# Up weights loaded by quarters into fixed places, the plain block split around the last products, six accumulating transfers for two blocks, and spilled forms read back later

## The chip, the cores and the metric

One core of a Trainium2 chip runs the whole kernel. The metric is device time in microseconds (us); lower is better. Engines are named as in the profile: PE (TensorE), DVE (VectorE), ACT (ScalarE), POOL (GpSimd), SP (SyncE, which here only issues transfers).

## The reference

One layer of a decoder trunk over 512 positions of width 1024: a mixer (mLSTM heads and a convolution group) and then a gated feed-forward block with a causal convolution of width 3. The change lies in the second half:

```
u  = rms_norm(x, ffn_pre_g) * (1 + sc2) + sh2          # 512 x 1024
up = causal_dwconv(u @ ffn_up, ffn_conv_w, ffn_conv_b)  # 1024 -> 2 * 2816, width 3 over positions
a, gt = split(up, 2)
f  = (silu(gt) * a) @ ffn_down                          # 2816 -> 1024
x  = x + g2 * rms_norm(f, ffn_post_g)
```

All is float32. sc2, sh2 and g2 are columns of a modulation that depends on c alone.

## The kernel before

A float32 product is made of three matmuls: each operand is split into a high and a low part (names ending in h and l), and high*high, high*low and low*high are summed (`mm3`, the lines L188 to L190; L1082 in `form_product`). A split is one ACT copy for the high part and a subtraction for the low part, on POOL in `w_split` (weights of the up stage) and on DVE in `split` (activations and down weights). `added_split` makes the low part otherwise: ACT writes the negated high part, and a transfer that POOL issues adds the source to it in place (an accumulating transfer).

**Up stage.** The 2816 hidden columns are 22 units of 128 (i = 0 to 21), each with a "value" and a "gate" block; two units make a pair m, 11 in all. Units 0 to 7 are plain: 48 matmuls of 512 columns. From unit 8 on, the even unit of a pair is a product unit: its blocks are computed by seven products of 12 matmuls of 256 columns (a Strassen-like scheme over halves of the positions and of the contraction), p1, p5, p7, p6 first and p2, p3, p4 last. Between the first four and the last three, DVE adds partial sums together (`u2`, then into the accumulators X and Z; L1106 to L1109), and p2, p3, p4 accumulate on top. The odd unit of the pair is plain, 48 matmuls of 512 columns in two halves (value, then gate), between the first four and the last three products. Before the weights can be multiplied, DVE forms sums of their four quarters in place (L1089, L1090, L1093 for p5, p7, p6; L1114 for p3). Weights for p1 to p7 are split by `w_split`; the plain unit's four by `added_split`. The position side of the products (`tforms`, t1 to t4) is made by `token_forms` after units 4 and 6.

Each unit's result goes through `conv3` (an ACT pass, two DVE passes), the silu and a product into F (L1146); `forms(m, F)` makes four sums (L1021 to L1024) and splits them (fh on ACT L1013, fl on DVE L1014) for the down stage, and sends two blocks to DRAM (`g2d`, L1031 and L1032, from ACT's queue). The forms of pairs 0 to 3 are written out to `own` and read back by 16 transfers of 256 KB on SP's queue before the down weights' first loads.

Up weights come in loads of 1 MB into `raws`, a ring of two tiles, with 20 tiles of split weights in `wpool`. `asides` puts two modulation columns (`ada_block`, a DVE pass of 1024 columns, L155) in front of units 4, 8, 12 and 16; they are ordered on DVE behind an earlier operation, `last_lo`.

**Down stage.** `load1(m)` brings 768 KB of down weights (into the ring's tiles for m = 0, 1, 4, 5, ..., named wd, into the place of u2h, named wdmore, for m = 2, 3, 6, 7, ...), `forms1(m)` makes sums and splits (L1222 to L1224, b_ and t_), and `prod1` runs 24 matmuls of 512 columns for each m.

SP and PE run in the order in which the code is written. The order on ACT, DVE and POOL is chosen by a scheduler when the program is built; each engine then runs its list strictly in order.

Of the kernel before, what the change touches and what calls it, by code (L numbers as in the profile page):

```python
# [25 lines left out]
NF = DFF // P  # L26
# [26 lines left out]
def decoder_layer(ctx, tc, w_glu0, x, xT, c, adaT, vecs, w_glu, w_qko, w_v0, w_v, w_out, w_up, w_down, out):  # L53
    nc = tc.nc
    V, S, G, PE = nc.vector, nc.scalar, nc.gpsimd, nc.tensor
# [41 lines left out]
    def cvbank(name):  # L97
        return cvpool[0].tile([P, T], F32, tag="cv", name=name)
# [48 lines left out]
    def ada_block(i, behind):  # L147

        if i % 6 < 4 and 24 <= i < 40:
            r = spare[0][:, 2 * (i % 6) : 2 * (i % 6) + 2, :].rearrange("p j t -> p (j t)")  # L150
        else:
            r = adas.tile([P, D], F32, tag="ada", name=f"ada_{i}")
        nc.scalar.dma_start(r, adaT[i // 2][:, (i % 2) * D : (i % 2 + 1) * D])
        junk = small.tile([P, D], BF16, tag="junk", bufs=1, name=f"junk_{i}")
        t = V.scalar_tensor_tensor(out=junk, in0=r, scalar=1.0, in1=cb, op0=ALU.mult, op1=ALU.mult, accum_out=mod[:, i : i + 1])  # L155
        tc.add_manual_dep(t.ins, behind.ins.name, mybir.DependencyInfo(mybir.DependencyClass.NoSync, mybir.DependencyReason.DATA),
                          reason="order on VectorE")
# [6 lines left out]
    def w_split(src, name, pool=None, tag="w", eng=None):  # L164

        n = src.shape[1]
        pool = pool or wpool
        hi = pool.tile([P, T], F32R, tag=tag, name=f"{name}h")
        lo = pool.tile([P, T], F32R, tag=tag, name=f"{name}l")
        S.activation(hi[:, :n], src, AF.Copy)  # L170
        (eng or G).tensor_tensor(out=lo[:, :n], in0=src, in1=hi[:, :n].bitcast(F32), op=ALU.subtract)  # L171
        return hi, lo

    def w_load(view, name, pool=None, tag="w"):

        n = view.shape[1]
        r = raws.tile([P, 2048], F32, tag="raw", name=name)
        nc.sync.dma_start(r[:, :n], view)
        return [w_split(r[:, a : min(a + T, n)], f"{name}_{a}", pool, tag) for a in range(0, n, T)]

    def blk(pieces, b):
        hi, lo = pieces[b // 4]
        a = (b % 4) * P
        return hi[:, a : a + P], lo[:, a : a + P]

    def mm3(ps, a, b, start, stop):

        PE.matmul(ps, a[0], b[0], start=start, stop=False)  # L188
        PE.matmul(ps, a[0], b[1], start=False, stop=False)  # L189
        PE.matmul(ps, a[1], b[0], start=False, stop=stop)  # L190
# [104 lines left out]
    _, _, u = u_tiles("u")  # L295
# [693 lines left out]
    def halves(z):  # L989
        return z.rearrange("p (h t) -> p h t", h=2)  # L990

    def conv3(ps, i, name):
        t = cvtile(f"{name}c")
        w = lambda tap: vcol("ffn_conv_w", tap * 44 + i)
        S.activation(t, ps, AF.Identity, bias=vcol("ffn_conv_b", i), scale=w(2))
        for d in range(1, 3):
            V.scalar_tensor_tensor(out=t[:, d:], in0=ps[:, : T - d], scalar=w(2 - d), in1=t[:, d:], op0=ALU.mult, op1=ALU.add)
        return t
# [60 lines left out]
            split(z, hi, lo)  # L1059
            tforms[n] += [tuple(y[:, h * HT : (h + 1) * HT] for y in (hi, lo)) for h in range(2)]  # L1060

    def up_load(i):
        r = raws.tile([P, 2048], F32, tag="raw", name=f"wup{i}")
        nc.sync.dma_start(r, w_up[i])
        return r

    def quarter(r, b):
        return r[:, b * T : (b + 1) * T]

    def added_split(r, i, q):  # L1070

        hi, lo = (wpool.tile([P, T], F32R, tag="w", name=f"wup{i}_{q}{n}") for n in "hl")
        S.activation(hi, quarter(r, q), AF.Copy)
        S.activation(lo, quarter(r, q), AF.Copy, scale=-1.0)
        G.dma_start(lo, quarter(r, q), accum_op=ALU.add)
        return hi, lo

    def form_product(ps, w, b, start, stop):
# [4 lines left out]

    def first_forms(i):

        r = up_load(i)
# [25 lines left out]
    def last_forms(i, r):  # L1112
        a11, a12, a22 = quarter(r, 0), quarter(r, 1), quarter(r, 3)
        V.tensor_tensor(out=a11, in0=a12, in1=a11, op=ALU.subtract)  # L1114
        return [w_split(z, f"wup{i}_{n}") for n, z in (("p2", a12), ("p3", a11), ("p4", a22))]

    def last_products_up(banks, w):
        X, Z = banks
# [1 line left out]
        form_product(X[:, HT:], w[1], B22, False, True)  # L1120
        form_product(Z[:, :HT], w[2], tforms["t4"], False, True)

    def plain_unit(i):
        if i < NE:
            return early[i]
        if i < SUNITS[0]:
            pieces = w_load(w_up[i], f"wup{i}")
            bank = mmbank
        else:
            r = up_load(i)  # L1130
            pieces = [added_split(r, i, q) for q in range(4)]
            bank = cvbank
        both = []
        for half in range(2):
            ps = bank(f"up{i}_{half}")
            for k in range(KT):
                mm3(halves(ps), blk(pieces, half * KT + k), (u2h[:, :, k, :], u2l[:, :, k, :]), k == 0, k == KT - 1)
            both.append(ps)
        return both

    def unit_out(i, banks, F):
        pa, pg = banks
        a = conv3(pa, i, f"fa{i}")
        g = conv3(pg, NF + i, f"fg{i}")
        S.activation(g, g, AF.Silu)
        V.tensor_tensor(out=F[:, (i % 2) * T : (i % 2 + 1) * T], in0=a, in1=g, op=ALU.mult)  # L1146

    def asides(i):
        if i in (4, 8, 12, 16):
            ada_block(38 + i // 2, last_lo[0])  # L1150
            ada_block(39 + i // 2, last_lo[0])
        if i == 18:
            ada_done(40, 48)
            gain(3, 40, "ffn_post_g")
            send_rows(3 * KT, KT)
            wide = adas.tile([P, D], F32, tag="ada", name="g2r")
            g2.append(row(3, lambda n: [wide[:, :T], wide[:, T:]], "g2"))

    g2 = []
    for m in range(NM):  # L1160
        F = vpool.tile([P, 2 * T + 8], F32, tag="vh", name=f"F{m}")
        i = 2 * m
        asides(i)
        if i in SUNITS:
            r, w = first_forms(i)
            banks = first_products(i, w)
            unit_out(i + 1, plain_unit(i + 1), F)
            last_products_up(banks, last_forms(i, r))
            unit_out(i, banks, F)
        else:  # L1170
            for i in (2 * m, 2 * m + 1):
                unit_out(i, plain_unit(i), F)
                if i in (4, 6):
                    token_forms(i // 2 - 2)
        forms(m, F)
        if m < SPILLED:
            for n, pair in enumerate(pairs[m]):
                for e, z in enumerate(pair):
                    nc.scalar.dma_start(own_d[m][:, (2 * n + e) * T : (2 * n + e + 1) * T], z.bitcast(F32))
    g2r = g2[0]  # L1180
    for m in range(SPILLED):
        pairs[m] = [(slot(f"fh{m}_{n}b", F32R), slot(f"fl{m}_{n}b", F32R)) for n in range(2)]
        for n, pair in enumerate(pairs[m]):
            for e, z in enumerate(pair):
                nc.sync.dma_start(z.bitcast(F32), own_d[m][:, (2 * n + e) * T : (2 * n + e + 1) * T])
    pairs = [pairs[m] for m in ORDER]
    g2_d = [g2_d[m] for m in ORDER]
    w_down = [w_down[m] for m in ORDER]

# [24 lines left out]
    def load1(m):  # L1214
        loaded[m] = r = wd_raw(m, 1)
        nc.sync.dma_start(r[:, T:], w_down[m][:, T:])
# [244 lines left out]
```

## Time and profile before

| | |
|---|---|
| median of 3 runs | 819.56 us (818.29 to 820.01) |
| profiled execution | 821.4 us, span 819.4 us |
| PE busy | 766.4 us, 94% |
| DVE busy | 648.2 us, 79% |
| ACT busy | 435.9 us, 53% |
| POOL busy | 380.9 us, 46% |
| moved by DMA | 141.12 MB, mean 172 GB/s |

Busy time is that of the engine's own instructions; issuing transfers is not counted. A wait in square brackets behind a row is the engine's idle time before it, with the operation that ended it. The pairs with a product unit run from 506.56 us to 683.76 us on PE, the down stage starts at 704.69 us.

### The profile page before, as it was taken

The numbers are of one execution on the slowest core, as the hardware profiler recorded it, in microseconds if no ns is written. First come the engines' busy times: TensorE is split into PE (matmuls) and PEld (weight loads), VectorE is DVE, ScalarE is ACT, GpSimd is POOL, SyncE is SP. The second block draws the span as 40 slices with busy tenths as digits, with TensorE's granted clock in tenths as the row PEclk, the third lists the DMA queues.
The fourth block names the chain that finished last, engine by engine and source line by source line (L and its number), as shares of the span: only waits on it lengthen the run. The fifth ranks groups of instructions, "written<-read, shape, count | busy, mean of one in ns | idle before, by whom it ended". The sixth has DMA issues, their size and how long they took to land.

```text
span 819.4 us, 11429 instructions
## 1 busy us (share of the span) xinstructions
PE 766.4 (94%) x3961; PEld 655.5 (80%) x3961; DVE 648.2 (79%) x1039; ACT 435.9 (53%) x832; POOL 380.9 (46%) x315
## 2 busy tenths in 40 slices
PE   7999999999999999999999998989888993699996
PEld 6788898788788889888899887878777883488885
DVE  6979999999998667569587998775656574699895
ACT  4556374866775465714453445555654462355762
POOL 2049495976986444428424776445544450000001
PEclk9999999999999999999999999899989998699998
DMA  9982223131133624268536653565444663877872
GB/s 331 368 290 84 104 82 146 47 109 52 52 130 130 204 102 156 102 226 314 202 132 233 224 174 103 192 174 148 91 137 146 174 157 107 310 279 235 292 245 103
DMA packets 45054, 141.12 MB, mean 172 GB/s; under 512 B 5154, under 2 KB 6594, under 8 KB 39108
## 3 DMA queue, kind: packets, MB, share of 16 engines
q1 hardware_dynamic: 26676, 100.37, 34.6%
q10 hardware_dynamic: 14288, 32.68, 11.2%
q0 software_dynamic: 4032, 7.34, 5.3%
q8 instruction: 31, 0.51, 0.3%
q14 instruction: 27, 0.22, 0.1%
HBM read 117.42 MB, written 15.61 MB: 162 GB/s over the span
## 4 chain that ended last, share of the span: by engine, by line
PE 56%; DVE 22%; DMA 10%; issue 5%; ACT 4%; POOL 2%; SPq 0%; ACTq 0%; DVEq 0%; POOLq 0%
DVE cv L731 10%; PE up L189 5%; PE up L188 4%; PE up L190 4%; PE p L1308 4%; DMA wup<-in_w_up 3%; PE glu L189 3%; PE glu L190 3%; DMA wup_3l<-wup 3%; PE glu L188 3%; PE p L188 3%; PE p L189 3%; PE p L190 3%; PE upx L1082 2%; PE mixa L188 2%
## 5 line engine op out<-in xcount | busy, mean ns | idle before, releaser
L731 DVE SCALAR_TENSOR_TENSOR cv<-gt,cvw,cv 128x505 f32<-128x505 f32 (+24 forms) x200 | 137.4, 729 | 2.3 <-ACT cv L719 1.1
L685 POOL TENSOR_TENSOR ro2r<-ro2t,mhalf 128x1 f32<-128x1 f32 x1 | 0.6, 559 | 132.1 <-DVE ro2t L683 132.1
L727 POOL TENSOR_TENSOR cs<-cs,cs 128x510 f32<-128x510 f32 (+3 forms) x32 | 41.8, 1305 | 0.3
L155 DVE SCALAR_TENSOR_TENSOR junk<-ada,cb 128x1024 bf16<-128x1024 f32 x20 | 30.3, 1516 | 8.5 <-DMA ada<-in_adaT 8.2
L725 ACT ACTIVATE cs<-gt,cvw 128x511 f32<-128x511 f32 (+4 forms) x40 | 27.4, 717 | 6.3 <-POOL cs L727 3.1
L171 POOL TENSOR_TENSOR wup_p1l<-wup,wup_p1h 128x512 fp32r<-128x512 f32 x7 | 9.6, 1376 | 38.5 <-ACT wup_p1h L170 38.5
L1014 DVE TENSOR_TENSOR fl<-F,fh 128x512 fp32r<-128x512 f32 x11 | 11.8, 1073 | 18.2 <-ACT fh L1013 18.2
L189 PE MATMUL up<-u2l,wup_0h 128*128 128x512 f32 (+1 forms) x72 | 25.7, 356 | 0.2 <-DVE u2l L910 0.2
L188 PE MATMUL up<-u2h,wup_0h 128*128 128x512 f32 (+1 forms) x72 | 25.6, 356 | 0.0
L190 PE MATMUL up<-u2h,wup_0l 128*128 128x512 f32 (+1 forms) x72 | 25.4, 353 | 0.0
L171 POOL TENSOR_TENSOR wqko_1024l<-wqko,wqko_1024h 128x512 fp32r<-128x512 f32 x12 | 16.3, 1359 | 18.4 <-ACT wqko_1024h L170 12.9
L171 POOL TENSOR_TENSOR wglu_0l<-wglu,wglu_0h 128x512 fp32r<-128x512 f32 x4 | 5.5, 1386 | 40.8 <-PE glu L190 40.5
L1082 PE MATMUL upx<-u2h,wup_p2h 128*128 128x256 f32 x28 | 9.6, 341 | 16.0 <-DVE upx L1109 9.3
L155 DVE SCALAR_TENSOR_TENSOR junk<-spare,cb 128x1024 bf16<-128x1024 f32 x12 | 19.0, 1586 | 3.4 <-DMA spare<-in_adaT 3.2
L188 PE MATMUL p<-b_0h,fh 128*128 128x512 f32 x2 | 1.4, 714 | 20.9 <-ACT b_0h L1013 20.9
L1082 PEld LDWEIGHTS upx<-u2h,wup_p2h 128*128 128x128 f32 x28 | 6.4, 227 | 18.0 <-ACT wup_p7h L170 7.7
L188 PE MATMUL qko<-uh,wqko_1024h 128*128 128x512 f32 x48 | 20.6, 430 | 0.0
L188 PE MATMUL qko<-uh,wqko_0h 128*128 128x512 f32 x48 | 20.2, 420 | 0.0
L171 POOL TENSOR_TENSOR wup_p5l<-wup,wup_p5h 128x512 fp32r<-128x512 f32 x7 | 9.0, 1282 | 24.0 <-ACT wup_p5h L170 24.0
L276 DVE SCALAR_TENSOR_TENSOR junk<-ada,cb 128x1024 bf16<-128x1024 f32 x16 | 19.5, 1218 | 0.1
L171 POOL TENSOR_TENSOR wo_512l<-wo,wo_512h 128x512 fp32r<-128x512 f32 x8 | 12.9, 1615 | 13.7 <-ACT wo_512h L170 13.7
L171 POOL TENSOR_TENSOR wqko_0l<-wqko,wqko_0h 128x512 fp32r<-128x512 f32 x12 | 16.6, 1384 | 4.9 <-ACT wqko_0h L170 4.8
(1205 smaller groups left out, 3208.3 us busy)
## 6 DMA issues: line engine op xcount, KB each, us to landing
wup<-in_w_up SPq DMA_DIRECT2D x22, 1024.0 KB, 6.9
wqko<-in_w_qko SPq DMA_DIRECT2D x12, 1024.0 KB, 4.8
ada<-in_adaT ACTq DMA_DIRECT2D x20, 512.0 KB, 5.1
ada<-in_adaT SPq DMA_DIRECT2D x16, 512.0 KB, 6.9
wo<-in_w_out SPq DMA_DIRECT2D x8, 1024.0 KB, 4.8
spare<-in_adaT ACTq DMA_DIRECT2D x12, 512.0 KB, 7.3
wd<-in_w_down SPq DMA_DIRECT2D x6, 768.0 KB, 6.4
g2kept<-g2d SPq DMA_DIRECT2D x11, 384.0 KB, 6.0
```

Source lines behind the costliest of these rows:

```text
L155: t = V.scalar_tensor_tensor(out=junk, in0=r, scalar=1.0, in1=cb, op0=ALU.mult, op1=ALU.mult, accum_out=mod[:, i : i + 1])
L171: (eng or G).tensor_tensor(out=lo[:, :n], in0=src, in1=hi[:, :n].bitcast(F32), op=ALU.subtract)
L188: PE.matmul(ps, a[0], b[0], start=start, stop=False)
L189: PE.matmul(ps, a[0], b[1], start=False, stop=False)
L190: PE.matmul(ps, a[1], b[0], start=False, stop=stop)
L276: V.scalar_tensor_tensor(out=junk, in0=first[k][:, i * D : (i + 1) * D], scalar=1.0, in1=cb, op0=ALU.mult, op1=ALU.mult, accum_out=part[k] ...
L725: S.activation(t[:, d:], cvx[j][:, : T - d], AF.Copy, scale=w(CK - 1 - d))
L727: G.tensor_tensor(out=side[:, d:], in0=side[:, d:], in1=t[:, d:], op=ALU.add)
L731: last_tap[0] = V.scalar_tensor_tensor(out=cp[:, d:], in0=cvx[j][:, : T - d], scalar=w(CK - 1 - d), in1=cp[:, d:], op0=ALU.mult, op1=ALU.add)
L1014: behind_turn(V.tensor_tensor(out=lo, in0=src, in1=hi.bitcast(F32), op=ALU.subtract))
L1082: PE.matmul(ps, x, y, start=start and k == 0 and n == 0, stop=stop and k == NT - 1 and n == 2, skip_group_check=True)
L1308: PE.matmul(ps[q], x, y, start=False, stop=m == NM - 1 and i == 2, skip_group_check=True)
```

## The change

- Units 8 and up are loaded by quarters of 256 KB, four transfers for one, into two tiles that belong to them (`wups`, one for even and one for odd units). The even unit's quarters come in the order 0, 2, 3, 1.
- The plain unit of a pair is split: its value half runs between the first four and the last three products, its gate half after the last three. The product unit's result is made before that of the plain unit.
- The splits for p2 and p4 become `added_split` too, so that a pair has six accumulating transfers (four before) and five subtractions on POOL (seven before).
- `token_forms` runs after units 3 and 4 instead of 4 and 6.
- The modulation columns are ordered behind the previous unit's product into F (`gated`) instead of `last_lo`.
- The 16 transfers that read the spilled forms back come after the first three `load1` on SP instead of before them.

```diff
-    def up_load(i):
-        r = raws.tile([P, 2048], F32, tag="raw", name=f"wup{i}")
-        nc.sync.dma_start(r, w_up[i])
-        return r
+    up_raw = []
+
+    def up_load(i, order):
+        if not up_raw:
+            up_raw.extend(raws.tile([P, 2048], F32, tag="raw", name=f"wups{n}") for n in range(2))
+        for q in order:
+            nc.sync.dma_start(quarter(up_raw[i % 2], q), quarter(w_up[i], q))
+        return up_raw[i % 2]
...
-        return [w_split(z, f"wup{i}_{n}") for n, z in (("p2", a12), ("p3", a11), ("p4", a22))]
+        return [added_split(a12, f"wup{i}_p2"), w_split(a11, f"wup{i}_p3"), added_split(a22, f"wup{i}_p4")]
...
+    def plain_half(ps, pieces, off):
+        for k in range(KT):
+            mm3(halves(ps), blk(pieces, off + k), (u2h[:, :, k, :], u2l[:, :, k, :]), k == 0, k == KT - 1)
+        return ps
...
-            ada_block(38 + i // 2, last_lo[0])
-            ada_block(39 + i // 2, last_lo[0])
+            ada_block(38 + i // 2, gated[0])
+            ada_block(39 + i // 2, gated[0])
...
-            r, w = first_forms(i)
-            banks = first_products(i, w)
-            unit_out(i + 1, plain_unit(i + 1), F)
-            last_products_up(banks, last_forms(i, r))
-            unit_out(i, banks, F)
+            j = i + 1
+            r, w = first_forms(i)
+            banks = first_products(i, w)
+            z = up_load(j, range(4))
+            pa = plain_half(cvbank(f"up{j}_0"), [added_split(quarter(z, q), f"wup{j}_{q}") for q in range(2)], 0)
+            ja = conv3(pa, j, f"fa{j}")
+            last_products_up(banks, last_forms(i, r))
+            unit_out(i, conv3(banks[0], i, f"fa{i}"), conv3(banks[1], NF + i, f"fg{i}"), F)
+            pg = plain_half(cvbank(f"up{j}_1"), [added_split(quarter(z, q), f"wup{j}_{q}") for q in range(2, 4)], 0)
+            unit_out(j, ja, conv3(pg, NF + j, f"fg{j}"), F)
...
-                if i in (4, 6):
-                    token_forms(i // 2 - 2)
+                if i in (3, 4):
+                    token_forms(i - 3)
...
     for m in range(3):
         load1(m)
+    for m in range(SPILLED):
+        reload(m)
```

How it moves instructions, at the places that the prediction speaks of. SP where the down stage begins: wd_0, wd_1 and wdmore are the first down weights, fh and fl the spilled forms. Before:

```order
L1185 DMA fl_0b<-own_4552 128x512
L1185 DMA fh_1b<-own_4552 128x512
L1185 DMA fl_1b<-own_4552 128x512
L1216 DMA wd_0_6842<-in_w_down 128x1536
L1216 DMA wd_1_6844<-in_w_down 128x1536
L1216 DMA wdmore<-in_w_down 128x1536
L1226 DMA t2d_4538<-wd_0_6842 128x512
L1216 DMA wdmore<-in_w_down 128x1536
```

and now:

```order
L1068 DMA wups_5123<-in_w_up 128x512 x4
L1220 DMA wd_0_6854<-in_w_down 128x1536
L1220 DMA wd_1_6856<-in_w_down 128x1536
L1220 DMA wdmore<-in_w_down 128x1536
L1188 DMA fh_0b<-own_4549 128x512
L1188 DMA fl_0b<-own_4549 128x512
L1188 DMA fh_1b<-own_4549 128x512
```

All 16 reads of own now stand between the third and the fourth load of down weights (the second wdmore, m = 3).

DVE between pair 14's F and what p2 of pair 16 needs (u_16 is `u2`, upx the accumulator X; junk are the modulation columns). Before:

```order
L1146 TENSOR_TENSOR F_5837<-fa14c,fg14c 128x512
L1021 TENSOR_TENSOR ysum<-F_5837 128x256
L1022 TENSOR_TENSOR F_5837<-F_5837 128x256
L1023 TENSOR_TENSOR ysum<-ysum,F_5837 128x256
L1024 TENSOR_TENSOR ysq<-F_5837,ysum 128x256
L1014 TENSOR_TENSOR fl_0_6064<-F_5837,fh_0_6063 128x512
L1089 TENSOR_TENSOR wup_6328<-wup_6328 128x512
L1014 TENSOR_TENSOR fl_1_6068<-ysum,fh_1_6067 128x512
L1090 TENSOR_TENSOR wup_6328<-wup_6328 128x512
L997 SCALAR_TENSOR_TENSOR fa17c<-up_0_6184,vec,fa17c 128x511
L1106 TENSOR_TENSOR u_16_6107<-upx_6103,p_16_6106 128x256
```

and now:

```order
L155 SCALAR_TENSOR_TENSOR junk_6102,mod<-ada_6100,cb 128x1024
L1021 TENSOR_TENSOR ysum<-F_5857 128x256
L1093 TENSOR_TENSOR wups_5122<-wups_5122 128x512
L155 SCALAR_TENSOR_TENSOR junk_6106,mod<-ada_6104,cb 128x1024
L1022 TENSOR_TENSOR F_5857<-F_5857 128x256
L1023 TENSOR_TENSOR ysum<-ysum,F_5857 128x256
L1094 TENSOR_TENSOR wups_5122<-wups_5122 128x512
L160 TENSOR_TENSOR mod<-mod,vec 128x8
L1024 TENSOR_TENSOR ysq<-F_5857,ysum 128x256
L1014 TENSOR_TENSOR fl_0_6090<-F_5857,fh_0_6089 128x512
L667 SCALAR_TENSOR_TENSOR gains<-mod,vec 128x8
L1014 TENSOR_TENSOR fl_1_6094<-ysum,fh_1_6093 128x512
```

The row behind the last is L1110, u_16. The two junk rows are new there, and the two sums of the next product unit's quarters (L1093 and L1094, before L1089 and L1090) stand wholly in front of u_16.

DVE at the same place for pair 20, the last one. Before:

```order
L1024 TENSOR_TENSOR ysq<-F_6317,ysum 128x256
L1014 TENSOR_TENSOR fl_0_6554<-F_6317,fh_0_6553 128x512
L1014 TENSOR_TENSOR fl_1_6558<-ysum,fh_1_6557 128x512
L997 SCALAR_TENSOR_TENSOR fa21c<-up_0_6666,vec,fa21c 128x511
L1106 TENSOR_TENSOR u_20_6589<-upx_6585,p_20_6588 128x256
```

and now:

```order
L1226 TENSOR_TENSOR wd_0_6854<-wd_0_6854 128x512
L1024 TENSOR_TENSOR ysq<-F_6349,ysum 128x256
L1014 TENSOR_TENSOR b_0l<-wd_0_6854,b_0h 128x512
L1227 TENSOR_TENSOR wd_0_6854<-wd_0_6854 128x512
L1014 TENSOR_TENSOR fl_0_6592<-F_6349,fh_0_6591 128x512
L1014 TENSOR_TENSOR fl_1_6596<-ysum,fh_1_6595 128x512
L1228 TENSOR_TENSOR wd_0_6854<-wd_0_6854 128x512
L1110 TENSOR_TENSOR u_20_6629<-upx_6625,p_20_6628 128x256
L1014 TENSOR_TENSOR t_0l<-wd_0_6854,t_0h 128x512 x2
L1111 TENSOR_TENSOR upz_6626<-upz_6626,u_20_6629 128x256
L1113 TENSOR_TENSOR upx_6625<-upx_6625,u_20_6629 128x256
```

The forms of the first down weights (L1226 to L1228 and the low parts b_0l and t_0l) now run among the forms of pair 18 and ahead of the sums that p2 of unit 20 waits for.

More of the change, by code (lines that the diff above doesn't have):

```diff
@@ L1060, in token_forms, with added_split @@
             tforms[n] += [tuple(y[:, h * HT : (h + 1) * HT] for y in (hi, lo)) for h in range(2)]
-    def up_load(i):
-        r = raws.tile([P, 2048], F32, tag="raw", name=f"wup{i}")
-        nc.sync.dma_start(r, w_up[i])
-        return r
+    up_raw = []
[5 more added lines that the diff above has]
+        return up_raw[i % 2]
     def quarter(r, b):
         return r[:, b * T : (b + 1) * T]
[L1070 to L1075, printed above, removed]
+    def added_split(src, name):
+        hi, lo = (wpool.tile([P, T], F32R, tag="w", name=f"{name}{n}") for n in "hl")
+        S.activation(hi, src, AF.Copy)
+        S.activation(lo, src, AF.Copy, scale=-1.0)
+        G.dma_start(lo, src, accum_op=ALU.add)
         return hi, lo
@@ L1084, in first_forms @@
     def first_forms(i):
-        r = up_load(i)
+        r = up_load(i, (0, 2, 3, 1))
         a11, a21, a22 = quarter(r, 0), quarter(r, 2), quarter(r, 3)
@@ L1125, in plain_unit, with unit_out @@
             return early[i]
[L1126 to L1144, printed above, removed]
+        pieces = w_load(w_up[i], f"wup{i}")
+        return [plain_half(mmbank(f"up{i}_{half}"), pieces, half * KT) for half in range(2)]
+    gated = [None]
+    def unit_out(i, a, g, F):
         S.activation(g, g, AF.Silu)
-        V.tensor_tensor(out=F[:, (i % 2) * T : (i % 2 + 1) * T], in0=a, in1=g, op=ALU.mult)
+        gated[0] = V.tensor_tensor(out=F[:, (i % 2) * T : (i % 2 + 1) * T], in0=a, in1=g, op=ALU.mult)
     def asides(i):
         if i in (4, 8, 12, 16):
-            ada_block(38 + i // 2, last_lo[0])
-            ada_block(39 + i // 2, last_lo[0])
+            ada_block(38 + i // 2, gated[0])
+            ada_block(39 + i // 2, gated[0])
         if i == 18:
@@ L1180, in decoder_layer, with reload @@
     g2r = g2[0]
-    for m in range(SPILLED):
-        pairs[m] = [(slot(f"fh{m}_{n}b", F32R), slot(f"fl{m}_{n}b", F32R)) for n in range(2)]
-        for n, pair in enumerate(pairs[m]):
+    def reload(m):
+        pairs.append([(slot(f"fh{m}_{n}b", F32R), slot(f"fl{m}_{n}b", F32R)) for n in range(2)])
+        for n, pair in enumerate(pairs[-1]):
             for e, z in enumerate(pair):
                 nc.sync.dma_start(z.bitcast(F32), own_d[m][:, (2 * n + e) * T : (2 * n + e + 1) * T])
-    pairs = [pairs[m] for m in ORDER]
+    pairs = pairs[SPILLED:]
     g2_d = [g2_d[m] for m in ORDER]
```

3 lines of the change are left out of this document (2 added, 1 removed).

## The prediction

> **What bounds the kernel now.** I read the page first, then the waits of TensorE over the stage that the change touches, then the timeline rows around those waits.
>
> ```profile
> span 819.4 us, 11429 instructions
> PE 766.4 (94%) x3961; PEld 655.5 (80%) x3961; DVE 648.2 (79%) x1039; ACT 435.9 (53%) x832; POOL 380.9 (46%) x315
> ```
>
> PE is busy for 94% of the span, so the most that can be won is PE's idle time, and it matters where that lies. The waits of PE between 430 and 720 us (total, times, longest):
>
> ```profile
> PE p L188 <- ACT b_0h L1013: 20.9, 1, 20.9
> PE upx L1082 <- DVE upx L1109: 9.3, 3, 4.0
> PE upx L1082 <- ACT wup_p5h L170: 6.7, 2, 3.7
> PE upx L1082 <- ACT t1h L1013: 1.8, 1, 1.8
> PE upx L1082 <- DVE t1l L1014: 1.5, 1, 1.5
> ```
>
> One hole of 20.9 us where the down stage starts, and 19.3 us in seven small ones inside the seven pairs (a product unit with its plain unit). PE's own rows give the pace and the borders (start, duration):
>
> ```profile
> 506.11 0.39 PE L189 MATMUL up<-u2l,wup_1536h 128*128 128x512 f32 x1
> 506.34 0.39 PE L190 MATMUL up<-u2h,wup_1536l 128*128 128x512 f32 x1
> 506.56 0.28 PE L1082 MATMUL upx<-u2h,wup_p1h 128*128 128x256 f32 x1
> 506.68 0.28 PE L1082 MATMUL upx<-u2l,wup_p1h 128*128 128x256 f32 x1
> 605.24 0.55 PE L1082 MATMUL upx<-u2h,wup_p2h 128*128 128x256 f32 x1 [3.99 <-DVE upx L1109]
> 605.59 0.42 PE L1082 MATMUL upx<-u2l,wup_p2h 128*128 128x256 f32 x1
> 605.81 0.41 PE L1082 MATMUL upx<-u2h,wup_p2l 128*128 128x256 f32 x1
> 683.48 0.28 PE L1082 MATMUL upz<-t4h,wup_p4l 128*128 128x256 f32 x1
> ```
>
> The pitch is 0.12 us for a 256-column matmul and 0.227 for a 512-column one, so a pair without waits costs 84 x 0.12 + 48 x 0.227 = 21.0 us. Seven pairs would take 147; from 506.56 to 683.76 (the last row's end) they took 177.2, which is 25.3 each. Of the 30.5 us lost, 19.3 are waits; the other 11.2 are slower running behind them: after the 3.99 us wait the pitch is 0.22 and not 0.12.
>
> What makes the period 25.3 us is a loop through the weight loads:
>
> ```profile
> 588.25 0.87 POOL L1075 DMA_DIRECT2D wup_3l<-wup  x1 [0.74 <-ACT wup_p2h L170]
> 593.23 1.83 SPq L1064 DMA_DIRECT2D wup<-in_w_up  x2
> 599.07 0.63 ACT L170 ACTIVATE wup_p1h<-wup 128x512 fp32r<-128x512 f32 x1 [4.00 <-DMA wup<-in_w_up]
> 600.25 1.38 DVE L1014 TENSOR_TENSOR fl<-F,fh 128x512 fp32r<-128x512 f32 x1 [2.74 <-ACT fh L1013]
> 602.75 0.41 DVE L1106 TENSOR_TENSOR u<-upx,p 128x256 f32<-128x256 f32 x1
> ```
>
> The plain unit's last accumulating transfer (issued 588.25) lands at about 593.2; only then may both 1 MB loads issue; ACT's next p1h waits for one; fh is queued behind p1h on ACT; fl waits for fh on DVE; the u sum (L1106) comes after fl; and p2 waits for that at 605.24.
>
> **The change, part by part.**
>
> *Quarters in fixed places.* This cuts the loop: a quarter of a tile can be loaded as soon as that quarter has been read. The new loop, from one p2 to the next: p2, p3, p4 and 12 matmuls of the plain unit's second half until the tiles for the p4 split come free, 36 x 0.12 + 12 x 0.227 = 7.0; two ACT copies 1.2 (0.6 each, like p1h above); issue and landing of p4's accumulating transfer; the fourth quarter's load; then on DVE two subtractions and fl (0.6 to 0.7 each) and three 256-column operations (0.4 each), 3.0. The transfers' rows (KB, median us to landing), all between 500 and 720 us but the last, which is the page's:
>
> ```profile
> wup_0l<-wup POOLq DMA_DIRECT2D x7, 256.0 KB, 3.4
> wup_3l<-wup POOLq DMA_DIRECT2D x7, 256.0 KB, 5.1
> own<-fl ACTq DMA_DIRECT2D x4, 256.0 KB, 2.3
> fh_0b<-own SPq DMA_DIRECT2D x4, 256.0 KB, 4.7
> wup<-in_w_up SPq DMA_DIRECT2D x12, 1024.0 KB, 6.9
> wd<-in_w_down SPq DMA_DIRECT2D x6, 768.0 KB, 6.4
> ```
>
> No quarter load of up weights exists before; its bounds are 2.3 and 4.7 us. The loop is then 7.0 + 1.2 + 3.4 + 2.3 + 3.0 = 16.9 at best and 7.0 + 1.2 + 5.1 + 4.7 + 3.0 = 21.0 at worst. The pair itself is 21.0, so by itself the loop stalls nothing, but the worst leaves no room.
>
> *What stands in that loop on DVE.* An operation on DVE with both inputs in SBUF gets longer beside a POOL subtraction:
>
> ```profile
> 589.18 3.06 DVE L1146 TENSOR_TENSOR F<-fa13c,fg13c 128x512 f32<-128x512 f32 x1
> 595.10 0.69 DVE L1146 TENSOR_TENSOR F<-fa12c,fg12c 128x512 f32<-128x512 f32 x1 [0.76 <-ACT fg12c L1145]
> 588.81 1.63 POOL L171 TENSOR_TENSOR wup_p2l<-wup,wup_p2h 128x512 fp32r<-128x512 f32 x1
> L171 POOL TENSOR_TENSOR wup_p5l<-wup,wup_p5h 128x512 fp32r<-128x512 f32 x7 | 9.0, 1282 | 24.0 <-ACT wup_p5h L170 24.0
> ```
>
> That is 2.4 us for one hit (3.06 for 0.69); a POOL subtraction by itself takes 1.3 (the last row, the page's: busy, then mean ns). Taking the upper loop, since its transfers will be as crowded as now, one hit on the chain is a wait of 2.4; it does not fall there each time, so I take half, 1.2, for pairs 10, 14 and 18: 3.6.
>
> *The modulation columns.* The eight L155 operations now follow the previous unit's F product, two at a time, ahead of the u sum of pairs 8, 12 and 16. Their row (ns min/median/max):
>
> ```profile
> L155 DVE SCALAR_TENSOR_TENSOR junk<-ada,cb x8: 1214/1438/1974, 433.6 to 461.0; 128x1024 bf16<-128x1024 f32 x8
> ```
>
> Two cost 2.9 us. Pairs 12 and 16: 1.2 + 2.9 = 4.1 each, 8.2. Where they run now, no wait of PE in the list above lies behind them, so I credit nothing there.
>
> *Pair 8.* In the new order p2 follows p1, p5, p7, p6 and only half of the plain unit: 506.56 + 48 x 0.12 + 24 x 0.227 = 517.8. Today DVE makes p2's inputs for that pair here:
>
> ```profile
> 527.08 0.42 DVE L1106 TENSOR_TENSOR u<-upx,p 128x256 f32<-128x256 f32 x1 [0.27 <-ACT p L1105]
> 527.95 0.42 DVE L1109 TENSOR_TENSOR upx<-upx,u 128x256 f32<-128x256 f32 x1
> ```
>
> With nothing else changed p2 would wait until 528.4, 10.6 us. The earlier token forms take the t1 waits (1.8 and 1.5) away and eight DVE operations out of this stretch (5.2), and two L155 come in: 10.6 - 5.2 + 2.9 = 8.3. The ends: 3.0, if a hit goes too and the L155 lie off the chain, and 13.5, if the eight were off it.
>
> *Pair 20.* Six of the first down weights' DVE operations (L1226, b_0l, L1227, L1228, two t_0l, 0.6 each) now precede the last of p2's inputs: 1.2 + 3.6 = 4.8.
>
> *Sum in the up stage.* Waits 3.6 + 8.2 + 8.3 + 4.8 = 24.9, against 19.3 before. Slow running behind them: at least four waits with 12 matmuls at 0.22 instead of 0.12, 4.8; in before's proportion (11.2 for 19.3) 14.5; middle 9.7. Up stage 147 + 24.9 + 9.7 = 181.6, which is 4.4 more than now: at the place where it waits, the change trades one late thing for another.
>
> *Two more accumulating transfers and two POOL subtractions fewer per pair* cost ACT two copies (1.2 us of a 21 us pair, and it is busy 53% of the span) and POOL nothing (0.9 of issue for 1.3 of subtraction): zero off the chain; the copies on the chain are counted above.
>
> *The reads later.* Now the reloads hold the first down loads back; before's SP rows:
>
> ```profile
> 691.19 0.32 SPq L1185 DMA_DIRECT2D fl_1b<-own  x1
> 695.18 0.38 SPq L1185 DMA_DIRECT2D fl_1b<-own  x1
> 695.74 0.99 SPq L1216 DMA_DIRECT2D wd<-in_w_down  x2
> ```
>
> With wd_0 and wd_1 first, their forms are made in pair 20 and the hole of 20.9 goes. What is late next is m = 3: SP first waits with m = 2's load for u2h, that is for the end of the up stage, then issues 16 reloads (nine rows from 691.19 to 695.18, 0.5 each: 8.0), then m = 3's load, 6.4 to landing, 2.0 for its first forms: 17 us behind the stage's end with the issue. PE comes to m = 3 after 3 x 24 x 0.227 = 16.3. That wait is 1 at the least. At the most a reload waits for a transfer, as these SP waits show:
>
> ```profile
> SPq L1185 <- DMA g2d<-ysq: 15.0, 3, 6.9
> SPq L1185 <- DMA g2d<-F: 13.9, 2, 8.3
> ```
>
> One such wait (8.3) makes it 9. The last pair's g2d stores are again under way just then, so I take 7. DVE gives the rest: pair 20's outputs, which ran alone before (6.5 us busy in the hole), now run beside the first forms, and it has little room there:
>
> ```profile
> 684.00:705.00 21.00, 0.31 (x1) 0.29 (x1) 6.52 (x13) 2.98 (x5) 0.00 (x0) 0.62 0.67 235
> 720.00:760.00 40.00, 40.00 (x178) 33.13 (x177) 36.98 (x63) 23.08 (x42) 0.00 (x0) 1.00 0.77 258
> ```
>
> (PE, PEld, DVE, ACT, POOL busy; granted clock; DMA share; GB/s.) DVE at 92%: 2 us of waits of a few tenths. The low clock behind the hole, 0.62 there, comes back behind the wait at m = 3 and cancels.
>
> Total: +4.4 - 20.9 + 7 + 2 = -7.5. The profiled execution took 821.4 (2.0 around its span), so 813.9; the median of the runs lies 1.8 below the profiled one: **812 us**.
>
> **Rivals.**
> *All covers hold.* Only pair 8 waits (8.3 and 1.2 of pace): up 156.5, 20.7 less; the tail as above: -20.7 - 20.9 + 7 + 2 = -32.6, **787**. For it: neither of the loop's two bounds lies over 21.0, and two POOL subtractions fewer can hit DVE. Against: today's fl waited 2.7 for ACT and then ran 1.4 instead of 0.7, and L155 and the down weights' forms now stand in the same line. The Trainium skill ("SBUF — State Buffer", shared port pair) says that a DVE operation with two SBUF inputs and a GpSimd operation that reads SBUF block each other for the whole instruction; the 3.06 us row agrees, and by that rule 14 subtractions fewer would win at most 14 x 1.3 = 18 us, an estimate.
>
> *The loop is longer than the pair, each time (slower).* Place: the fourth quarter's load, ahead of u on DVE. If the worst transfers, a hit (2.4) and ACT's fh being late as in the row above (2.7) fall together, the period is 26.1, and pair 8 waits 10.6: up 32.8 + 6 x 26.1 + 2 x 2.9 + 3.6 = 198.8, +21.6; tail -20.9 + 9 + 2: **831**. It decides from an up stage of about 187 on (26.7 a pair), where the tail's gain is used up. For it: DVE order and four issues for one. Against: 256 KB rows land in 2.3 to 5.1, 1 MB in 6.9. The Trainium skill ("DMA: Bandwidth & Descriptors", Bandwidth) advises 1 MiB or more for each transfer, which speaks for this rival; no run here yet shows an up load of 256 KB, and the down stage draws 258 GB/s, more than a pair needs.
>
> *The tail gives nothing back.* The reloads meet both late transfers (8.3 + 6.9) and m = 3 waits 16: 4.4 - 20.9 + 16 + 2 = +1.5, **821**.
>
> **How the numbers follow.** Forecast 0.56 (804 to 818 by its own bounds: pair 8 at 3.0 or 13.5, pace at 4.8 or 14.5, m = 3 at 1 or 9, not all at one end), all covers hold 0.12, loop too long 0.20, no tail gain 0.12 (a third of it slower by over 0.2%, which is about what a measurement of this kernel can tell from no change). So faster 0.68, the first two; slower 0.20 + 0.04 = 0.24; same 0.08. The range 796 to 824 leaves out most of the second case and the upper part of the third.
>
> **What would show it.** In the changed trace: no wait of PE at the first b_0h; a wait of PE in the down stage's first 25 us, for b_3 or DVE behind wdmore; waits at p2 of pairs 8, 12, 16 and 20 longer than at 10, 14, 18; ACT's p1h without a 4 us wait for a load. Wrong I am if pairs run at 21 to 22 us (then far faster), or if p2 waits over 4 us in pairs without L155 (then slower).

## The result, and the profile after

The changed kernel takes 828.08 us (median of 4 runs, 826.08 to 830.35) against 819.78 for the one before: ratio 1.0106, 95% interval 1.0072 to 1.0139. It is slower by about 1%; the forecast was 812 and faster. Its profiled execution has a span of 828.6 us, 9.2 longer than before.

TensorE's waits from 430 us on (total, times, longest) say where. (In the rows of this document, SPq, ACTq and POOLq mark transfers that the engine issues; the time of such a row is the issue, not the transfer.)

```profile
PE upx L1086 <- DVE upx L1113: 33.1, 6, 14.1
PE p L188 <- ACT b_3h L1013: 9.1, 1, 9.1
PE upx L1086 <- ACT fa11c L995: 3.9, 1, 3.9
PE p L188 <- DVE fg21c L997: 0.5, 1, 0.5
PE upz L1086 <- DVE fg6c L997: 0.2, 1, 0.2
```

The hole of 20.9 us at the first b_0h is gone, and 9.1 came back at m = 3. The waits inside the seven pairs grew from 19.3 us, 16.0 of them at p2, to 37.0, all at p2. PE's rows show which pairs, and the border to the down stage:

```profile
532.15 0.55 PE L1086 MATMUL upx<-u2h,wup_p2h 128*128 128x256 f32 x1 [14.12 <-DVE upx L1113]
559.60 0.55 PE L1086 MATMUL upx<-u2h,wup_p2h 128*128 128x256 f32 x1 [3.92 <-ACT fa11c L995]
587.50 0.55 PE L1086 MATMUL upx<-u2h,wup_p2h 128*128 128x256 f32 x1 [4.42 <-DVE upx L1113]
636.08 0.36 PE L1086 MATMUL upx<-u2h,wup_p2h 128*128 128x256 f32 x1 [3.93 <-DVE upx L1113]
662.56 0.36 PE L1086 MATMUL upx<-u2h,wup_p2h 128*128 128x256 f32 x1 [3.66 <-DVE upx L1113]
692.03 0.55 PE L1086 MATMUL upx<-u2h,wup_p2h 128*128 128x256 f32 x1 [6.76 <-DVE upx L1113]
704.19 0.39 PE L190 MATMUL up<-u2h,wup_3l 128*128 128x512 f32 x1
704.42 0.39 PE L188 MATMUL p<-b_0h,fh 128*128 128x512 f32 x1
730.78 0.79 PE L188 MATMUL p<-b_3h,fh 128*128 128x512 f32 x1 [9.14 <-ACT b_3h L1013]
```

These are pairs 8, 10, 12, 16, 18, 20; pair 14 hardly waits (0.2 us). The first pair starts at 506.20, so the up stage lasts 198.2 us, 21.0 more than before. The balance closes: +21.0 in the up stage, -20.9 at the hole, +9.1 at m = 3, together +9.2, which is the difference of the spans.

The loop that I worked out for the forecast can be read, for one turn, from the p2 of pair 16 (636.08, above) to that of pair 18 (662.56):

```profile
645.70 0.62 ACT L1077 ACTIVATE wup_p4h<-wups 128x512 fp32r<-128x512 f32 x1
646.22 0.62 ACT L1078 ACTIVATE wup_p4l<-wups 128x512 fp32r<-128x512 f32 x1
647.25 1.07 POOL L1079 DMA_DIRECT2D wup_p4l<-wups  x1
654.92 1.38 SPq L1068 DMA_DIRECT2D wups<-in_w_up  x3
659.73 0.69 DVE L1094 TENSOR_TENSOR wups<-wups 128x512 f32<-128x512 f32 x1 [2.46 <-DMA wups<-in_w_up]
660.34 0.69 DVE L1014 TENSOR_TENSOR fl<-ysum,fh 128x512 fp32r<-128x512 f32 x1
661.14 0.40 DVE L1110 TENSOR_TENSOR u<-upx,p 128x256 f32<-128x256 f32 x1
661.99 0.42 DVE L1113 TENSOR_TENSOR upx<-upx,u 128x256 f32<-128x256 f32 x1
```

From p2 to p4's copies 9.6 us, the copies and the way to POOL 1.6, the accumulating transfer until SP goes on 7.7, the quarter's load until DVE goes on 4.8, DVE to the next p2 2.8: 26.5 us, against 21.0 that a pair takes on PE. It is not the same each time: from p2 to p2 the five turns from pair 8 to pair 18 took 27.5, 27.9, 23.4, 25.2 and 26.5 us, 26.1 in the mean. In the short one, which ends at pair 14, DVE's L1094 did not wait for a load. SP's waits from 500 to 735 us name p4's transfer too (first row, total, times, longest). The transfers in that stretch (KB, median us to landing):

```profile
SPq L1068 <- DMA wup_p4l<-wups: 31.9, 6, 6.4
wups<-in_w_up SPq DMA_DIRECT2D x48, 256.0 KB, 5.6
wup_p4l<-wups POOLq DMA_DIRECT2D x7, 256.0 KB, 6.6
wup_3l<-wups POOLq DMA_DIRECT2D x7, 256.0 KB, 6.0
```

### The profile page after: what moved, and what is told of

Same layout as the page of the kernel before. It is cut to its first block, busy times and chain, and to the rows that moved or that the text cites. A ratio compares the mean times of both kernels' runs of the same rounds, so it can differ in the third digit from the quotient of the medians.

```text
span 828.6 us, 11531 instructions
## 1 busy us (share of the span) xinstructions
PE 769.2 (93%) x3961; PEld 656.9 (79%) x3961; DVE 642.3 (78%) x1039; ACT 444.9 (54%) x846; POOL 372.9 (45%) x315
## 4 chain that ended last, share of the span: by engine, by line
PE 56%; DVE 20%; DMA 10%; issue 6%; ACT 4%; POOL 2%; SPq 0%; ACTq 0%; DVEq 0%; POOLq 0%
DVE cv L731 10%; PE up L189 4%; PE up L190 4%; PE up L188 4%; PE p L1314 4%; PE upx L1086 4%; DMA wup_p4l<-wups 3%; PE glu L189 3%; PE glu L188 3%; PE glu L190 3%; DMA wups<-in_w_up 2%; PE glu L316 2%; PE p L189 2%; PE p L188 2%; PE p L190 2%
## 5 line engine op out<-in xcount | busy, mean ns | idle before, releaser
L1086 PE MATMUL upx<-u2h,wup_p2h 128*128 128x256 f32 x28 | 11.3, 405 | 37.0 <-DVE upx L1113 33.1
L171 POOL TENSOR_TENSOR wup_p5l<-wups,wup_p5h 128x512 fp32r<-128x512 f32 x7 | 9.0, 1292 | 52.3 <-ACT wup_p5h L170 46.1
L189 PE MATMUL up<-u2l,wup_0h 128*128 128x512 f32 (+1 forms) x72 | 25.7, 356 | 0.2 <-DVE u2l L910 0.2
L171 POOL TENSOR_TENSOR wqko_1024l<-wqko,wqko_1024h 128x512 fp32r<-128x512 f32 x12 | 15.5, 1293 | 18.3 <-ACT wqko_1024h L170 12.9
L1013 ACT ACTIVATE fh<-F 128x512 fp32r<-128x512 f32 x11 | 6.9, 628 | 27.3 <-DVE F L1022 14.1
L171 POOL TENSOR_TENSOR wo_512l<-wo,wo_512h 128x512 fp32r<-128x512 f32 x8 | 12.9, 1617 | 13.4 <-ACT wo_512h L170 13.4
L190 PE MATMUL qko<-uh,wqko_1024l 128*128 128x512 f32 x48 | 18.8, 392 | 0.0
L190 PE MATMUL qko<-uh,wqko_0l 128*128 128x512 f32 x48 | 18.8, 391 | 0.0
```

The costliest lines, as they stand in the source:

```text
L1086: PE.matmul(ps, x, y, start=start and k == 0 and n == 0, stop=stop and k == NT - 1 and n == 2, skip_group_check=True)
```

## The experiments

Theory A: p2's inputs stand too far back in the lines of ACT and DVE (modulation passes, transfers that ACT issues, the first down weights). Theory B: the loop through p4's accumulating transfer and the fourth quarter's load is longer than a pair. The tail (m = 3) is a question of its own. All ratios are to the kernel before on the same chip, whose median there was 821.4 to 821.8 us; the changed kernel's is 1.0106. Spans are those of the profiled executions. The changed kernel's profiled execution took 830.35 us, 2.3 more than its median, so a difference of spans against it can be some 2 us off.

### The modulation passes early (e1)

```diff
-            ada_block(38 + i // 2, gated[0])
+            ada_block(38 + i // 2, last_lo[0])
```

(and the line after it likewise.)

> The changed kernel, but the eight modulation passes (L155) and their transfers are ordered behind last_lo again, as before the change, and so run ahead of the product pairs. Theory A (what PE waits for at p2 stands in line on ACT and DVE: L155 and the transfers that ACT issues for it): the wait at p2 of pair 8 falls from 14.1 us to 5 to 8, those of pairs 12 and 16 from 4.4 and 3.9 to under 1.5; with the slow running behind them the time falls by 10 to 16 us, to 812 to 818. Theory B (the loop through p4's accumulating transfer and the fourth quarter's load is longer than a pair): pairs 12 and 16 still wait 3 to 4 us as pairs 10 and 18 do, only pair 8 falls by the two passes, 2.4 us; the time falls by 2 to 5 us.

Measured: 822.96 us, ratio 1.0013 (0.9991 to 1.0035), span 821.7. The waits at p2:

```profile
532.10 0.55 PE L1086 MATMUL upx<-u2h,wup_p2h 128*128 128x256 f32 x1 [10.38 <-DVE upx L1113]
557.41 0.36 PE L1086 MATMUL upx<-u2h,wup_p2h 128*128 128x256 f32 x1 [2.83 <-ACT fa11c L995]
582.47 0.35 PE L1086 MATMUL upx<-u2h,wup_p2h 128*128 128x256 f32 x1 [2.35 <-ACT fa13c L995]
607.71 0.35 PE L1086 MATMUL upx<-u2h,wup_p2h 128*128 128x256 f32 x1 [2.52 <-ACT fa15c L995]
631.00 0.36 PE L1086 MATMUL upx<-u2h,wup_p2h 128*128 128x256 f32 x1 [2.06 <-ACT fa17c L995]
655.38 0.55 PE L1086 MATMUL upx<-u2h,wup_p2h 128*128 128x256 f32 x1 [3.04 <-DVE upx L1113]
```

With the passes gone the pairs 10 to 18 all wait 2.1 to 3.0 us, pair 14 too, which had hardly waited. That is a loop's picture, Theory B; the rows stand 23.3 to 25.3 us apart. Pair 8 fell by 3.7 and the span by 6.9, both between the two expectations; pairs 12 and 16 wait 2.4 and 2.1, less than Theory B said and more than Theory A. The passes do cost time, also where they now run: the pairs start 3.0 us later, at 509.22. But they were not why the ordinary pair waits.

### p2 and p4, or p4 alone, split on POOL again (e2, e6)

```diff
-        return [added_split(a12, f"wup{i}_p2"), w_split(a11, f"wup{i}_p3"), added_split(a22, f"wup{i}_p4")]
+        return [w_split(a12, f"wup{i}_p2"), w_split(a11, f"wup{i}_p3"), w_split(a22, f"wup{i}_p4")]
```

e6 changes p4 alone.

> The changed kernel, but p2 and p4 are split by POOL subtractions again: four accumulating transfers for a pair. Theory B: p4's low part is ready 1.3 us after its high part instead of 6.6 us after the issue, the fourth quarter's load is issued about 5 us earlier, DVE's L1094 no longer waits for it, and the waits of pairs 10 and 18 (3.9 and 3.7 us) fall under 1; the time falls by 8 to 12 us. Theory A: these waits stay within 1.5 us, the time changes by less than 3 us, or grows because two more POOL subtractions lengthen DVE operations.

> The changed kernel, but p4 alone is split by a POOL subtraction again, p2 still by an accumulating transfer (five for a pair). If the gain of 13.7 us with both back on POOL comes from the loop through p4's transfer (6.6 us) to the fourth quarter's load: the time is within 3 us of 814. If p2's transfer, or the number of them, matters as much: the time is 819 or more.

Measured: e2 814.39 us, ratio 0.9899 (0.9868 to 0.9930), span 813.2; e6 817.14 us, ratio 0.9960 (0.9943 to 0.9978), span 815.0. Of 15.4 us of span, p4 alone brings 13.6; by the ratios to before it is 12.0 of 17.0. So p4 is most of it, though e6's time is just outside the 3 us around 814, and e2 won more than the 8 to 12 expected. In e2:

```profile
555.89 0.36 PE L1086 MATMUL upx<-u2h,wup_p2h 128*128 128x256 f32 x1 [1.42 <-ACT wup_p7h L170]
579.38 0.36 PE L1086 MATMUL upx<-u2h,wup_p2h 128*128 128x256 f32 x1 [2.25 <-DVE upx L1113]
625.95 0.36 PE L1086 MATMUL upx<-u2h,wup_p2h 128*128 128x256 f32 x1 [2.42 <-DVE upx L1113]
wups<-in_w_up SPq DMA_DIRECT2D x48, 256.0 KB, 4.1
```

Pairs 14 and 18 wait 0.2, pair 10 waits 1.4, and only 12 and 16, which have the modulation passes in line, wait more. In e2 and in e6 DVE's L1094 waits for no load in any of the turns from pair 8 to pair 18. In e6 these five turns take 23.7 us in the mean, so 12.0 of its 13.6 us are won there. The quarter's load itself became 1.5 us faster (4.1 for 5.6). This settles it for pairs 10 to 18: Theory B made the steady wait, and the transfer that closes the loop is p4's. What remains at pairs 12 and 16 is Theory A's share (e12 below).

### The loads in one piece (e5)

```diff
-        for q in order:
-            nc.sync.dma_start(quarter(up_raw[i % 2], q), quarter(w_up[i], q))
+        nc.sync.dma_start(up_raw[i % 2], w_up[i])
```

> The changed kernel, but the up weights of each unit from 8 on come in one load of 1 MB into the fixed place instead of four of 256 KB. Theory B (loop: p4's accumulating transfer, then the load, then DVE): the load now has to wait for the same transfer and lands in 6.9 instead of 5.6 us, so pairs 10 to 18 wait about 1 us longer each (15.9 to 21) and the time grows by 4 to 10 us. Rival (it is the number of transfers that hurts: four issues for one on SP, transfers that ACT issues queued behind them, which held fh for 14.6 us in three places): those holds on ACT go, pairs 8 and 12 wait 5 us less each, and the time falls by 8 us or more.

Measured: 840.16 us, ratio 1.0235 (1.0200 to 1.0271), span 838.7, so 10.1 worse than the changed kernel, at the upper end of what Theory B said; the waits of pairs 10 to 18 came to 25.7 us, more than its 21. SP's waits from 500 to 720 us name the transfer:

```profile
SPq L1067 <- DMA wup_p4l<-wups: 138.2, 6, 28.7
SPq L1067 <- DMA wup_3l<-wups: 34.0, 6, 9.6
```

Loading by quarters is therefore a good part of the change, worth some 10 us beside the rest of it. p4's transfer itself landed in 3.9 us here instead of 6.6, but the whole megabyte now waits for it. The rival fails: no wait of ACT's fh is put down to a load here, and yet pair 8 waits 13.4 and pair 12 10.9 us.

### The reads (e3, e4)

e3 spreads them in the changed kernel:

```diff
-    for m in range(SPILLED):
-        reload(m)
     for m in range(NM):
...
+        if m < SPILLED:
+            reload(m)
```

The second pair of lines stands behind `load1(m + 3)` and `load_g2(m)`. e4 takes the kernel before and makes only the change's move, the reads behind the first three `load1`.

> The changed kernel, but each of the four spilled pairs is read back after one of the next four loads of down weights (behind load1(3) and on) instead of all 16 transfers in front of load1(3). If the wait of 9.1 us at m = 3 is the 16 reads standing in front of that load on SP: the wait goes to under 2 us and the time falls by 7 to 9 us, to 819 to 821. Rival (DVE, 92% busy in the steady down stage and with pair 20's outputs still to make, is what is late): a wait of 4 us or more remains among m = 2 to 5, and the time falls by less than 5 us.

> The kernel before with one part of the change alone: the reads of the spilled forms behind the first three loads of down weights. If the tail's part works by itself as in the changed kernel: the up stage stays at 177 us, the hole of 20.9 us at the first b_0h goes to under 3, a wait of 8 to 10 appears at m = 3, the time falls by 8 to 13 us, to 807 to 812. Rival (the down weights' loads find their ring tiles free only when the last pair has read its up weights, so they are as late as now): a hole of 8 us or more stays at the first b_0h beside the wait at m = 3, and the time falls by less than 4 us.

Measured: e3 819.23 us, ratio 0.9966 (0.9949 to 0.9983), span 818.0; no wait is left at m = 3, whose load SP issues at 701.85 here and at 722.26 in the changed kernel. e4 821.26 us, ratio 1.0006 (0.9980 to 1.0031), span 817.5: no gain, though by neither of the ways that I had written down. Its PE waits in the last pair and behind it:

```profile
687.61 0.55 PE L1082 MATMUL upx<-u2h,wup_p2h 128*128 128x256 f32 x1 [8.32 <-DVE upx L1109]
693.23 0.28 PE L1082 MATMUL upz<-t4h,wup_p4l 128*128 128x256 f32 x1
719.10 0.80 PE L188 MATMUL p<-b_3h,fh 128*128 128x512 f32 x1 [9.24 <-ACT b_3h L1013]
```

The hole of 20.9 us went whole, the up stage ended 9.7 us later (693.51; 683.76 before), with a new wait of 8.3 in pair 20, and 9.2 appeared at m = 3. So the move by itself gives nothing: what it takes from the start of the down stage it gives to pair 20, where the first down weights' forms now stand in front, and to the fourth load.

### Three pairs spilled (e7)

```diff
-    SPILLED = 4
+    SPILLED = 3
```

> The changed kernel, but the forms of pair 3 stay in SBUF: three pairs are written out and read back (12 reads, and no stores by ACT between pair 3's forms and unit 8's p15). If ACT's issue of these four stores holds the copies that DVE's sum for p2 of pair 8 needs: that wait falls from 14.1 us by 4 to 7. If it is the load loop or DVE there: by less than 2. The wait at m = 3 falls by the four reads, 2 us, in either case. Time 828 less 6 to 9, or less 2 to 4.

Measured: 817.55 us, ratio 0.9949 (0.9923 to 0.9976), span 815.9. Pair 8's wait fell from 14.1 to 8.6 and that at m = 3 from 9.1 to 7.0, as expected; the time fell more than the 6 to 9 expected (the span by 12.7): the up stage also lost 3.4 us of slow running and 0.9 of other waits. The changed kernel's ACT rows in pair 8, with the DVE row that writes fh's input, show the queue that this shortens; PE had been ready for p2 since 518.0:

```profile
519.53 3.80 ACTq L153 DMA_DIRECT2D ada<-in_adaT  x2
521.51 0.41 DVE L1022 TENSOR_TENSOR F<-F 128x256 f32<-128x256 f32 x1
523.38 0.63 ACT L1013 ACTIVATE fh<-F 128x512 fp32r<-128x512 f32 x1 [6.75 <-DMA wups<-in_w_up]
525.01 0.33 ACTq L1181 DMA_DIRECT2D own<-fh  x1
525.39 0.63 ACT L1013 ACTIVATE fh<-ysum 128x512 fp32r<-128x512 f32 x1 [1.38 <-DMA wups<-in_w_up]
527.08 0.33 ACTq L1032 DMA_DIRECT2D g2d<-ysq  x1
527.72 0.33 ACTq L1181 DMA_DIRECT2D own<-fl  x1
528.14 0.40 ACTq L1181 DMA_DIRECT2D own<-fh  x1
529.65 0.33 ACTq L1181 DMA_DIRECT2D own<-fl  x1
530.02 0.38 ACT L1106 ACTIVATE p<-upx 128x256 f32<-128x256 f32 x1 [4.00 <-DMA g2d<-ysq]
530.30 0.38 ACT L1109 ACTIVATE p<-upw 128x256 f32<-128x256 f32 x1
```

The two fh and the two p15 copies (p) are computations that need no transfer. Most of the first fh's 6.75 us is not the queue's doing: DVE, behind the two modulation passes, writes its input F only until 521.92, so the issue of the second ada holds it for 1.5 at the most. The second fh and p15 wait 1.38 and 4.00 us because a store in front of them on ACT's queue waits for another transfer. In e7, without four of these stores, the first fh starts 0.7 us earlier and p15 5.7 us earlier (524.30), and 5.5 us of pair 8's wait are gone.

### The plain unit whole again (e9)

```diff
+            pg = plain_half(cvbank(f"up{j}_1"), ...)
             last_products_up(banks, last_forms(i, r))
             unit_out(i, conv3(banks[0], i, f"fa{i}"), conv3(banks[1], NF + i, f"fg{i}"), F)
-            pg = plain_half(cvbank(f"up{j}_1"), ...)
```

> The changed kernel, but the plain unit is not split: both its halves run between the first four and the last three products, as before the change. If the single late things (pair 8's and pair 20's sums for p2) are what the split exposes: p2 comes 24 matmuls, 5.4 us, later in its pair, and the waits of pairs 8 and 20 fall from 14.1 and 6.8 by about 5 each, the others (3.7 to 4.4) little, because the load loop takes as long wherever p2 stands: time 815 to 821. If the split is what shortens the loop (half of the plain unit's tiles free only after p4): pairs 10 to 18 wait more than now, and the time is 826 or more.

Measured: 834.17 us, ratio 1.0153 (1.0120 to 1.0186), span 832.0. A miss in the time for the first expectation, half right in the picture; the time is in the second one's range, but not by its reason. Pair 8 waits 9.1, 5.0 less, as expected; pairs 10 to 18 together 15.5, as with the split (15.9): the loop takes as long wherever p2 stands. But pair 20 waits 12.1 instead of 6.8, and PE waits 2.4 us at the start of the down stage. The up stage is as long as with the split (507.45 to 705.08, 197.6 us). The DVE rows show why pair 20 lost what pair 8 won: DVE waits 5.4 us there for the first down load (L1226 at 684.35) and runs 13 operations of the first two down loads before the X sum at 698.05; with the split it was six.

### Together (e8, e10, e11, e12)

e8 is e2 and e3. e10 adds an order on ACT and DVE alone: the forms of the first two down loads come behind unit 20's p15 copies and its X sum (`after_op` is an order without a wait, as in `ada_block`).

```diff
-        V.tensor_tensor(out=t3, in0=b22, in1=b12, op=ALU.subtract)
+        after_op(V.tensor_tensor(out=t3, in0=b22, in1=b12, op=ALU.subtract), lastx[0], "order on VectorE")
...
+        if early_down[0]:
+            after_op(c, lastp[0], "order on ScalarE")
+            after_op(s, lastx[0], "order on VectorE")
```

e11 adds `SPILLED = 3`, e12 the early modulation passes.

> Two edits together: p2 and p4 split by POOL subtractions, and the reads spread behind the next four loads of down weights. If the two losses are separate, the gains add: 828.1 less 13.7 less 8.9 is 805.5; expected 803 to 808, which beats both kernels. If the shorter up stage only lets the down stage wait elsewhere (for loads, or for DVE): 809 or more.

> The combination of e8, and the forms of the first two down loads ordered behind unit 20's sums on DVE and behind its p15 copies on ACT. If these forms, made early, are what p2 of unit 20 waits for: its wait of 5.6 us falls to under 1.5, the down stage starts without a new wait, and the time falls by 5 to 7 us from 806.7, to 800 to 802. If the forms are then late for the down stage: a wait of 3 us or more appears at b_0 or b_1 and the time is 804 or more.

> The same as e10 with three pairs spilled instead of four. If ACT's stores of pair 3 hold p15 of pair 8 here too (5.1 us on a store in e8): that wait falls from 13.1 to 7 to 9, and the time by 4 to 7 us from e10's. If not: less than 2.

> The same as e11 with the modulation passes back behind last_lo, ahead of the product pairs. In e8 only pairs 12 and 16, where two passes stand in line, still wait (2.3 and 2.4), pairs 14 and 18 do not. If it is these passes: both waits go to under 0.5, pair 8's falls by 2 to 4, the pairs' start is some 3 us later, and the time falls by 4 to 7 us from e11's. If the passes only fill DVE time that is lost anyway: less than 2.

| | median us | ratio to before (95%) | span |
|---|---|---|---|
| e8 | 806.68 | 0.9823 (0.9804 to 0.9842) | 804.8 |
| e10 | 798.82 | 0.9727 (0.9704 to 0.9751) | 797.0 |
| e11 | 794.32 | 0.9665 (0.9637 to 0.9693) | 792.2 |
| e12 | 788.14 | 0.9596 (0.9570 to 0.9623) | 785.1 |

The losses were mostly separate: e2 and e3 took 15.4 and 10.6 us off the span, e8 both together 23.8, and its time is the one expected. e10's order took pair 20's wait (5.6 in e8) away whole; 5.0 us of another one, which neither expectation had, appeared behind the up stage's end, at the matmul with t_0h. Still 7.8 us of span were won: pair 20 took 21.0 us instead of 29.2 and pair 8 1.5 less, the pairs started 0.8 later, and all from the first b_0h on took 1.1 longer. e11 and e12 came out as expected (pair 8 at 7.8 and 5.8, pairs 12 and 16 at 0.2). In e12 the waits from 430 us on are

```profile
PE upx L1097 <- ACT fa9c L995: 5.8, 1, 5.8
PE p L188 <- DVE fg21c L997: 4.2, 1, 4.2
PE upx L1097 <- DVE fa6c L997: 1.7, 1, 1.7
PE upx L1097 <- DVE upx L1124: 1.2, 5, 0.3
```

Pairs 10 to 18 run without a wait of over 0.4 us, and the kernel is 4.0% faster than the one before. Pair 8 still waits 5.8, the down stage's start 4.2.

## Why the prediction was wrong

- **The hole at b_0h**: right, all 20.9 us went. **m = 3**: named rightly with its cause, 16 reads in front of the load, and one late transfer; 7 forecast, 9.1 measured, 9 was the upper bound. The 2 us of small waits in the down stage came to 0.5, so the tail as a whole was forecast within 1 us. SP issued the first read at 704.99 and the m = 3 load at 722.26, with 6.9 us of it waiting for a g2d store. e3 shows it is this.
- **The new loop**: the step that failed. It was put at 16.9 to 21.0 us, "so by itself the loop stalls nothing". It is 26.5 in the rows above, 5.5 more than its upper bound, and 26.1 in the mean. Two terms made this: p2 to p4's copies 9.6 instead of 7.0 (the slow running behind p2's wait lies in it too), and p4's accumulating transfer 7.7 to the load's issue, 6.6 by its median, instead of at most 5.1, taken from transfers that had fewer beside them. The fourth quarter's load took 4.8 in that turn, about its upper bound of 4.7, and 5.6 by the median of all. I had taken the rows of a machine with four accumulating transfers and two loads for each pair as the bound for one with six and eight. By e6 p4's transfer alone was worth 13.6 us of span. Why it lands later than the 5.1 was not tested; along POOL's row of issues in a pair the medians rise (wup_0l 3.4, wup_1l 3.9, wup_p2l 4.3, wup_p4l 6.6).
- **The pairs without modulation passes**: 1.2 us each forecast, as an occasional collision on DVE; pairs 10 and 18 waited 3.9 and 3.7, pair 14 0.2. Their cause is the loop, by e1, e2 and e6, not the collision. The sign of being wrong that I had set, over 4 us, was not reached: it was too high.
- **Pairs 12 and 16**: 4.1 forecast, 4.4 and 3.9 measured. Right in size, by luck: the passes explain only the part that e2 leaves, 2.3 and 2.4, and the loop the rest.
- **Pair 8**: 8.3 forecast, at most 13.5, measured 14.1. The price of two DVE passes was counted; that the transfers issued by ACT stand in front of the second fh and of p15 there, and wait themselves, was not. e7 and e1 took 5.5 and 3.7 off.
- **Pair 20**: 4.8 forecast, 6.8 measured, in the place named. The forms cost more than their own time since their first one waits for its load: ACT's b_0h waited 7.8 us for it and DVE's L1226 6.2, with p15 and the u sum queued behind. e10, which changes that order alone beside e8, shows that it was the cause.
- **Up stage in sum**: 181.6 forecast, 198.2 measured: 12.1 us more of waits (37.0 for 24.9) and, over 147, 14.2 us of slower running instead of 9.7. (177.2 less 147 is 30.2 and not 30.5, which changes nothing; but not all of what the waits leave is slow running, as in e12 pairs with waits of 0.2 still take 21.4 us and not 21.0.) The rival "the loop is longer than the pair, each time" had 198.8 for it, with a period of 26.1; four of the six later pairs took 26.4 to 27.6 from first product to first product. It gave 831 us; 828 came. Its place was right, its terms were not: DVE's operations in the turn above are not lengthened (0.69 us) and fh is not what is late, so that 198.8 and 198.2 agree so closely is luck. It had a chance of 0.20, too little: the upper bound of the loop already equalled the pair's time on PE, so any term that was a little larger had to become a wait in each pair. The rival "all covers hold" counted two POOL subtractions fewer as a possible gain; e2 has them back and is 15.4 us of span faster.
- **The rule on sizes of transfers** that I set beside that rival ("DMA: Bandwidth & Descriptors", Bandwidth, in the Trainium skill) spoke for what came nearest, but not for the reason at work: loads of 1 MB in the same place cost 10.1 us more (e5), although they moved more for their time (1 MB in 6.5 us, 256 KB in 5.6). What counted here is when the tile that a load fills may be overwritten, not the rate.

## What to carry to other kernels

A transfer that frees a buffer for the next load lies in the loop of that buffer: write down the whole loop with the transfers as crowded as they will be, and when its upper bound only equals the engine's period, expect a wait in every turn. Of several edits in one change, try each alone: here quarters were good, p4's accumulating transfer bad, and reads moved later worth nothing until the load behind them and the order in the last pair were moved too. A wait that is removed at the start of a stage comes back at the next thing in the same queue, so look one entry further there before counting the gain.

## What the runs showed of the hardware that was not expected

- In the median a load of 256 KB took 5.6 us with six accumulating transfers for a pair, 4.4 with five (e6) and 4.1 with four (e2), a load of 1 MB in e5 6.5. The accumulating transfers were no fixed price either: the plain unit's last one took 5.1 before, 6.0 in the changed kernel and 8.1 in e8, whose pairs 14 and 18 waited only 0.2 all the same.
- A transfer that ACT issues can hold ACT's computations behind it while it waits for another transfer, whose data they do not use: in pair 8 the second fh waited 1.38 us, put down to a load that SP had issued, and p15 4.00 us, put down to a store of ACT's own.
- PE does not always run slowly behind a wait, nor always at once: behind 3.92 us (559.60) the matmuls followed each other at 0.21 us from the start, behind 3.66 us (662.56) eight ran at 0.12 first and then 16 at 0.21, 1.5 us lost in all, and in e1 behind 2.52 us (607.71) none ran slowly. Over the waits at p2 in all traces, no slow stretch followed one of under 2.0 us, one followed each of 3.03 us and more, and of those between some.
